# Loading all token tiles at once and reordering the opening of a fused recurrent, attention and expert block

## The chip, the cores and the metric

The kernel runs on one core of a Trainium2 chip. A core has five instruction queues: TensorE (PE in the profile, with its weight loads as PEld), VectorE (DVE), ScalarE (ACT), GpSimd (POOL) and SyncE (SP, which here only issues DMAs). The metric is the device time of one execution in microseconds, the median of three runs.

## The reference, cut to what matters

One layer over 1024 tokens of width 1024, in float32:

```python
u = rms_norm(h, norm_mix_g)
proj = u @ w_in                 # 1024 x 5152
x_rnn, g_rnn, q_c, kv_c, k_pe, gate_logits = split(proj)
A = rg_lru(causal_conv(x_rnn)) * gelu(g_rnn)
B = mla(q_c, kv_c, k_pe, positions)      # rope on a part of q and k
h = h + (sigmoid(gA) * A + sigmoid(gB) * B) @ w_out
h = h + hier_moe(rms_norm(h))            # top-2 of 8 experts in the best of 4 groups
```

The change touches only the opening: reading h, normalizing it, the first columns of `u @ w_in`, and the cosine and sine tables that rope uses later.

## The kernel before

Every float32 operand of a matmul is held as a high and a low part: `split` casts the value to the short form on ScalarE and subtracts the cast from the value on VectorE. A product is three matmuls (high by high, low by high, high by low). The instructions are put in order per engine by a list scheduler: program order is the priority among those that are ready, and each engine then runs its list strictly in that order. `tc.issue_after(i)` adds one constraint to that: what the block traces on the engine of `i` stands behind `i` in that engine's list.

**The opening (L332 to L396).** The tokens come in eight tiles of 128 rows. `load_x` fetches one tile (SP queue) into one of four buffers `xt`, so tile 4 waits until tile 0 has been scaled. `prepare` squares and sums it on ScalarE (L343) and takes the reciprocal root with a dozen tiny VectorE instructions (`rsqrt`, L80 to L87). `turn_tile` scales the tile by root and gain (L353 on VectorE; for tiles 5 and 7 L350 on ScalarE and L351 on GpSimd), transposes it on TensorE in eight blocks (L358), and splits it into `uh` and `ul` (both at L96). From tile 2 on the transposes share one PSUM buffer, tag `po`.

**The three begun projections.** `begin` loads 128 columns of `w_in` and splits them; for the first two the subtraction runs on GpSimd (`by=G`). `start_part(c0, q)` runs the 24 matmuls of 128x256 (L164) of one projection over the tokens of tiles 2q and 2q+1. The order is: for each q, projection 0, a tile, projection 1, a tile, projection 2. So quarter q of all three waits for tiles 2q and 2q+1. The last quarter runs in `proj_ft`.

**The rope tables (`rope_tables`, L284 to L330).** They are 27 VectorE instructions, nearly all in one chain, on 128x128 numbers or fewer, one transpose on TensorE and two sines on ScalarE. They stand in program order behind the first two `prepare` calls. Their scratch pool `wR` is released after the opening.

**What follows.** Scratch pool `wS` takes the place of `wR` and of the opening's pool; its last buffer, `tz`, covers nearly all of what `wR` held. The rest of the latent projections run (L169 to L171, then k_pe at L505, small sums at L476 and L512), while VectorE builds the Strassen sums of `u` (`u_sums`, L207 to L215 and L96), 28 instructions of 128x1024 that begin when tile 7 is split. Their results `t1` to `t4` are the operands of the products in `pair` (L245), which begin behind L512. `t1h`, `t1l`, `t2h`, `t2l` have 8 KB per partition each and are unused before that.

Of the kernel before, what the change touches and what calls it, by code (L numbers as in the profile page):

```python
# [10 lines left out]
F32 = mybir.dt.float32  # L11
F32R = mybir.dt.float32r
BF16 = mybir.dt.bfloat16
I32 = mybir.dt.int32
AF = mybir.ActivationFunctionType
OP = mybir.AluOpType
# [3 lines left out]
P = 128  # L20
T = 1024
D = 1024
NT = T // P
# [15 lines left out]
def block_kernel(ctx: ExitStack, tc, a, out):  # L39
    nc = tc.nc  # L40
    V, S, G, TE = nc.vector, nc.scalar, nc.gpsimd, nc.tensor
# [4 lines left out]
    def bcast_row(ap1, n):  # L46
        return bass.AP(tensor=ap1.tensor, offset=ap1.offset, ap=[[0, P], [1, n]])
# [25 lines left out]
    def rsqrt(dst, src, shape, pool):  # L73

        n = int(np.prod(shape))
        view = lambda t: t if len(shape) == 1 else t.rearrange("p (a b) -> p a b", a=shape[0])
        gi = pool.tile([P, n], I32, tag=f"rsi{n}", name="rs_i")
        tt = pool.tile([P, n], F32, tag=f"rst{n}", name="rs_t")
        g3, t, y = view(gi), view(tt), view(gi.bitcast(F32))
        V.tensor_scalar(g3, src.bitcast(I32), 1, -1, op0=OP.arith_shift_right, op1=OP.bitwise_xor)  # L80
        V.tensor_tensor(gi, gi, magic[:, :n], op=OP.add)
        if n == 1:
            hs = pool.tile([P, 1], F32, tag="rsh", name="rs_h")
            V.tensor_scalar(hs, src, -0.5, None, op0=OP.mult)
            for it in range(3):
                V.scalar_tensor_tensor(t, y, y, hs, op0=OP.mult, op1=OP.mult)
                V.scalar_tensor_tensor(dst if it == 2 else y, t, 1.5, y, op0=OP.add, op1=OP.mult)  # L87
            return
        for it in range(3):
            V.tensor_tensor(t, y, y, op=OP.mult)  # L90
            V.scalar_tensor_tensor(t, t, -0.5, src, op0=OP.mult, op1=OP.mult)
            V.scalar_tensor_tensor(dst if it == 2 else y, t, 1.5, y, op0=OP.add, op1=OP.mult)

    def split(hi, lo, src, by=V):

        return S.copy(hi, src), by.tensor_tensor(lo, src, hi.bitcast(F32), op=OP.subtract)  # L96
# [13 lines left out]
    up = tc.alloc_tile_pool(name="up", bufs=1, reuse_waits="tile")  # L110
    uh = [up.tile([P, KD, 512], F32R, name=f"uh{i}") for i in range(2)]
    ul = [up.tile([P, KD, 512], F32R, name=f"ul{i}") for i in range(2)]
    K4 = KD // 2
    psW = tc.alloc_tile_pool(name="psW", bufs=3, space=PSUM, reuse_waits="tile")
# [10 lines left out]
    def bank(nm="ps"):  # L125
        return bank2(nm)[:, 0] if psA is None else psA.tile([P, 512], F32, tag="ps", name=nm)
# [20 lines left out]

    begun = {}

    def proj_weights(c0, by=V):  # L150
        st = raw_tile().rearrange("p (k f) -> p k f", k=KD)
        nc.sync.dma_start(st, w_in_v[:, :, c0:c0 + P])
        b0 = 3 + 2 * (turn[2] % 3)
        turn[2] += 1
        wh, wl = (new(b0 + n, F32R).rearrange("p (k f) -> p k f", k=KD) for n in range(2))
        split(wh, wl, st, by)
        return wh, wl

    def proj_part(ps, w, hf, sl):
# [13 lines left out]
    def proj_ft(c0, done):  # L173
        if c0 in begun:
            ps, w = begun.pop(c0)
            proj_part(ps, w, 1, slice(256, 512))
        else:
            w = proj_weights(c0)
            ps = bank2()
            proj_half(ps, w, 0)  # L180
            proj_half(ps, w, 1)
        done(ps.rearrange("p h t -> p (h t)"))
# [8 lines left out]
    ub = {}  # L191

    def u_sums(pool):

        for nm in ("t1", "t2", "t3"):
            ub[nm] = tuple(up.tile([P, K4, 512], F32R, name=f"{nm}{q}") for q in "hl")
        for nm, h, k in (("b11", 0, 0), ("b21", 0, K4), ("b22", 1, K4), ("t4", 1, 0)):
            ub[nm] = tuple([t[h][:, k:k + K4] for t in (uh, ul)])
        b12 = ub["t4"]
        f = lambda t, s: t[:, s].bitcast(F32)  # L200
        for k in range(0, K4, 2):
            s = slice(k, k + 2)
            tmp = lambda nm: pool.tile([P, 2, 512], F32, tag=nm, name=nm, bufs=1)

            def minus(nm, a, b):
                x, y = tmp(nm), tmp("ty")
                V.tensor_tensor(x, f(a[0], s), f(b[0], s), op=OP.subtract)  # L207
                V.tensor_tensor(y, f(a[1], s), f(b[1], s), op=OP.subtract)
                V.tensor_tensor(x, x, y, op=OP.add)
                return x  # L210

            def less(nm, a, x):
                y = tmp(nm)
                V.tensor_tensor(y, f(a[0], s), x, op=OP.subtract)
                V.tensor_tensor(y, y, f(a[1], s), op=OP.add)  # L215
                return y

            x3 = minus("tx", ub["b22"], b12)
            split(*(t[:, s] for t in ub["t3"]), x3)
            x1 = minus("tz", b12, ub["b11"])  # L220
            split(*(t[:, s] for t in ub["t1"]), x1)
            x2 = less("tx", ub["b22"], x1)
            split(*(t[:, s] for t in ub["t2"]), x2)
            x4 = less("tz", ub["b21"], x2)
            split(*(t[:, s] for t in ub["t4"]), x4)
# [56 lines left out]
    wR = tc.alloc_tile_pool(name="wR", bufs=1, side="right", reuse_waits="tile")  # L282

    def rope_tables(w0):  # L284
# [5 lines left out]
        gqk = w0.tile([P, 2, DQ], F32, name="gqk")  # L290
        for i, nm in enumerate(("q_norm_g", "k_norm_g")):
            nc.scalar.dma_start(gqk[:, i, :], bcast_row(a[nm], DQ))
        pp2 = bank("pp2")[:, :NT]
        TE.transpose(pp2, posf, ident[:NT, :NT])
        pos = w0.tile([P, NT], F32, name="pos")
        V.tensor_copy(pos, pp2)
# [35 lines left out]
    with tc.tile_pool(name="wA", bufs=4, side="right", reuse_waits="tile") as wA:  # L332
        gmix = wA.tile([P, D], F32, name="gmix", bufs=1)
        xts, rs = {}, {}

        def load_x(i):
            xts[i] = wA.tile([P, D], F32, tag="xt", name="xt")
            nc.sync.dma_start(xts[i], x[i * P:(i + 1) * P, :])

        def prepare(i):  # L340
            ss, rs[i] = (wA.tile([P, 1], F32, tag=nm, name=nm) for nm in ("ss", "rs"))
            xns[i] = wA.tile([P, D], F32, tag="xn", name="xn")
            S.activation(xns[i], xts[i], AF.Square, scale=D ** -0.5, accum_out=ss)  # L343
            V.tensor_scalar(ss, ss, EPS, None, op0=OP.add)
            rsqrt(rs[i], ss, [1], wA)

        def turn_tile(i, tag):
            xn, r = xns[i], rs[i]
            if i % 2 and i > 3:
                S.activation(xn, xts[i], AF.Copy, scale=r)  # L350
                G.tensor_tensor(xn, xn, gmix, op=OP.mult)  # L351
            else:
                V.scalar_tensor_tensor(xn, xts[i], r, gmix, op0=OP.mult, op1=OP.mult)  # L353
            hh, ii = divmod(i, 4)
            pt = psW.tile([P, 2, 512], F32, tag=tag, name="pt", bufs=1 if tag == "po" else 3)
            pt = pt.rearrange("p h (c t) -> p (h c) t", c=4)
            for k in range(KD):
                TE.transpose(pt[:, k], xn[:, k * P:(k + 1) * P], ident)  # L358
            split(uh[hh][:, :, ii * P:(ii + 1) * P], ul[hh][:, :, ii * P:(ii + 1) * P], pt)

        def begin(c0, by):
            begun[c0] = [None, proj_weights(c0, by=by)]

        def start_part(c0, q):
            if begun[c0][0] is None:
                begun[c0][0] = psW.tile([P, 2, 512], F32, tag="ps", name="pp")
            proj_part(*begun[c0], q // 2, slice(256 * (q % 2), 256 * (q % 2) + 256))

        xns = {}
        first = (C_Q, C_Q + P, C_Q + 2 * P)  # L370
        load_x(0)
        load_x(1)
        nc.sync.dma_start(gmix, bcast_row(a["norm_mix_g"], D))
        for i in range(2):
            prepare(i)
        begin(first[0], G)
        rope_tables(wR)
        for i in range(2):
            turn_tile(i, "ps")
            load_x(2 + i)  # L380
        for i in range(2, 4):
            prepare(i)
        begin(first[1], G)
        begin(first[2], V)
        for i in range(4, NT):
            load_x(i)
        for q in range(3):
            for n, c0 in enumerate(first):
                start_part(c0, q)
                if n < 2:  # L390
                    turn_tile(2 * q + 2 + n, "po")
            if q < 2:
                for i in range(2):
                    prepare(2 * q + 4 + i)

    wR.release()  # L396

# [81 lines left out]
    with tc.tile_pool(name="wS", bufs=2, side="right", reuse_waits="tile") as wS:  # L479
# [20 lines left out]
        ps = bank2()  # L500
# [17 lines left out]
    with tc.tile_pool(name="wD", bufs=1, side="right", reuse_waits="tile") as wD:  # L518
# [7 lines left out]
        for fp in range(4):  # L526
            fs = [2 * fp, 2 * fp + 1]
            c0 = 2 * P * fp
# [4 lines left out]
            for j, ft in enumerate(fs):  # L533
                y = wD.tile([P, T], F32, tag="y", name="y", bufs=2)
# [19 lines left out]
            for j, ft in enumerate(fs):  # L554
                for w in range(2):
                    ps = [bank("psl") for _ in range(2)]
# [1037 lines left out]
```

## Time and profile before

| | |
|---|---|
| time, three runs | 1417.18, 1420.1, 1422.19 us (median 1420.1) |
| the profiled execution | 1418.82 us, its span 1417.1 us |
| busy in the span | PE 95%, PEld 77%, DVE 77%, ACT 55%, POOL 27% |
| mean granted TensorE clock | 0.979 |

The span is what the engines recorded; 1.7 us lie around it. A group of rows below is one view of that one execution, with times in microseconds from the start of the span. Instructions on one engine overlap a little: a 128x1024 VectorE instruction that lasts 1.22 is followed by the next 1.13 later.

### The profile page before, as it was taken

To read this page: it belongs to the slowest core of one execution; us is meant where nothing else is said; L and a number is where in the kernel's file an instruction comes from. 1 tells how busy PE (TensorE), PEld (TensorE's weight loads), DVE (VectorE), ACT (ScalarE), POOL (GpSimd) and SP (SyncE) were. 2 spreads that over 40 slices of the span, in tenths; PEclk is the share of its full clock that TensorE was granted. 3 is DMA by queue.
4 is the path that set the end of the run, shared out by engine and by line. 5 is a ranking of instruction groups with operands and counts; after the bars stand their busy time and mean duration, and the time that the engine had idled before them with its cause. 6 is when DMAs were issued, how large, how long until landed. Compare 5 with 4: busy or idle time off the path is not lost.

```text
span 1417.1 us, 20382 instructions
## 1 busy us (share of the span) xinstructions
PE 1344.1 (95%) x7371; PEld 1094.3 (77%) x7372; DVE 1090.0 (77%) x1894; ACT 783.0 (55%) x1138; POOL 382.0 (27%) x313
## 2 busy tenths in 40 slices
PE   5999999999999899998999999998995999999995
PEld 4967888888888788987655555557874999999995
DVE  7698878787966655678577777785496899999894
ACT  5444747565734353423444444444532888888884
POOL 2100000000000211221777777550422222222222
PEclk9999999999999899999999999999997999999998
DMA  6112222222353545643434444363567899999962
GB/s 216 49 59 87 89 75 89 75 90 89 134 178 120 178 173 172 174 148 99 116 100 117 107 120 132 107 220 134 198 233 250 289 379 381 380 380 379 368 175 36
DMA packets 119945, 244.32 MB, mean 172 GB/s; under 512 B 32636, under 2 KB 68564, under 8 KB 119840
## 3 DMA queue, kind: packets, MB, share of 16 engines
q1 hardware_dynamic: 101768, 194.37, 40.9%
q0 software_dynamic: 17616, 48.46, 11.1%
q8 instruction: 59, 0.97, 0.3%
q14 instruction: 46, 0.38, 0.1%
q10 hardware_dynamic: 456, 0.14, 0.0%
HBM read 203.87 MB, written 55.83 MB: 183 GB/s over the span
## 4 chain that ended last, share of the span: by engine, by line
PE 83%; DVE 11%; DMA 2%; ACT 2%; issue 1%; POOL 0%; SPq 0%; POOLq 0%; DVEq 0%; ACTq 0%
PE pw L245 22%; PE pg L1442 13%; PE po L971 6%; PE py L1479 6%; PE pq L787 6%; PE ph L1172 4%; PE psm L923 3%; PE psl L560 3%; PE pss L953 3%; PE pss L955 2%; PE pss L954 2%; PE pt L1424 2%; PE pp L164 2%; PE pk L705 2%; PE pv L764 1%; DVE s L96 1%
## 5 line engine op out<-in xcount | busy, mean ns | idle before, releaser
L96 ACT CAST s<-s 128x1024 fp32r<-128x1024 f32 (+4 forms) x392 | 337.9, 882 | 179.8 <-PE pw L245 39.7
L96 DVE TENSOR_TENSOR s<-s,s 128x1024 fp32r<-128x1024 f32 (+3 forms) x384 | 382.5, 1023 | 52.8 <-ACT s L96 47.4
L1442 PE MATMUL pg<-s,s 128*128 128x256 f32 x1536 | 196.3, 284 | 0.7 <-DVE s L96 0.7
L1442 PEld LDWEIGHTS pg<-s,s 128*128 128x128 f32 x1536 | 189.8, 191 | 3.5 <-DVE s L96 0.9
L245 PE MATMUL pw<-uh,s 128*128 128x512 f32 x576 | 183.0, 392 | 0.0
L956 ACT ACTIVATE s<-pss 128x512 f32<-128x512 f32 (+4 forms) x192 | 90.1, 493 | 148.6 <-PE pss L955 144.9
L976 POOL TENSOR_TENSOR s<-s,s 128x896 f32<-128x896 f32 (+6 forms) x108 | 149.8, 1406 | 58.3 <-ACT s L956 40.8
L245 PEld LDWEIGHTS pw<-uh,s 128*128 128x128 f32 x576 | 108.8, 189 | 23.9 <-ACT s L96 0.9
L924 DVE TENSOR_REDUCE mx<-psm 128x1 f32<-128x320 f32 (+4 forms) x192 | 94.5, 547 | 41.1 <-PE psm L923 40.7
L245 PE MATMUL pw<-ul,s 128*128 128x512 f32 x288 | 112.7, 391 | 0.0
L971 PE MATMUL po<-s,s 128*64 128x512 f32 (+3 forms) x384 | 106.8, 507 | 0.3 <-ACT s L956 0.3
L1172 PE MATMUL ph<-s,s 128*128 128x512 f32 x384 | 98.3, 404 | 3.5 <-ACT s L96 2.9
L787 PE MATMUL pq<-s,cqh 128*128 128x384 f32 x384 | 99.2, 337 | 0.0
L1479 PE MATMUL py<-s,hT 128*128 128x512 f32 x384 | 96.2, 399 | 1.2 <-ACT hT L96 1.2
L1485 POOL DMA_INDIRECT out_dram<-s,idx x32 | 54.7, 1709 | 121.6 <-ACT s L1484 107.4
L1172 PEld LDWEIGHTS ph<-s,s 128*128 128x128 f32 x384 | 70.6, 191 | 19.5 <-ACT s L96 4.1
L1479 PEld LDWEIGHTS py<-s,hT 128*128 128x128 f32 x384 | 69.8, 188 | 15.1 <-ACT hT L96 1.4
L953 PE MATMUL pss<-s,s 128*128 128x512 f32 (+4 forms) x192 | 72.9, 380 | 3.0 <-ACT s L956 3.0
L1416 POOL DMA_INDIRECT s<-xs,idx x32 | 35.7, 1117 | 131.2 <-PE pt L1424 107.1
L953 PEld LDWEIGHTS pss<-s,s 128*128 128x128 f32 x192 | 36.4, 189 | 44.0 <-DVE mx L924 17.0
L787 PEld LDWEIGHTS pq<-s,cqh 128*128 128x128 f32 x384 | 69.2, 188 | 1.1 <-DVE vt L768 0.8
L955 PE MATMUL pss<-s,s 128*128 128x512 f32 (+4 forms) x192 | 65.8, 343 | 0.0
(389 smaller groups left out, 2603.8 us busy)
## 6 DMA issues: line engine op xcount, KB each, us to landing
s<-in_w_gate_dram SPq DMA_DIRECT2D x64, 512.0 KB
s<-in_w_up_dram SPq DMA_DIRECT2D x63, 512.0 KB
s<-in_w_down_dram SPq DMA_DIRECT2D x63, 512.0 KB
s<-in_w_in_dram SPq DMA_DIRECT2D x40, 512.0 KB
s<-rk_d SPq DMA_DIRECT2D x16, 384.0 KB
q_d<-qt POOLq DMA_DIRECT2D x8, 768.0 KB, 4.7
s<-q_d SPq DMA_DIRECT2D x16, 384.0 KB
s<-in_w_uq_dram SPq DMA_DIRECT2D x12, 384.0 KB
```

The source lines that it names most:

```text
L96: return S.copy(hi, src), by.tensor_tensor(lo, src, hi.bitcast(F32), op=OP.subtract)
L245: TE.matmul(ps[at], w[:, l, k], ub[b][m][:, k], start=(go and k == 0 and n == 0), stop=(k == K4 - 1 and n == 2), skip_group_check=True)
L787: TE.matmul(p2[:, t % 2, :384], l[:, k, i * P:(i + 1) * P], wq[k // 2][r][:, k % 2], start=(k == 0 and n == 0), stop=(k == 5 and n == 2))
L924: V.tensor_reduce((mx[:, j, R1 + i:R1 + i + 1], mx2[:, j, i:i + 1])[b], ps[:, :cn], axis=AX.X, op=OP.max, negate=True)
L953: TE.matmul(o[:, :cn], kh[:, ks], qh[:, q], start=True, stop=False)
L955: TE.matmul(o[:, :cn], kh[:, ks], ql[:, q], start=False, stop=True)
L956: S.activation(pT[:, b * cn:(b + 1) * cn], o[:, :cn], AF.Exp)
L971: TE.matmul(po[pp][s][j * DV:(j + 1) * DV, lo - s * 512:], va[:, c, j, :], pTs[j][:, lo - c * P:hi - c * P], start=(c == 0), stop=(c == 4 ...
L976: (V if pp == NP - 1 and j == 0 and c < 5 else G).tensor_tensor(ac, ac, pTs[j][:, :T - c * P], op=OP.add)
L1172: TE.matmul(o, m2[l][:, k], wo[c][k // 2][r][:, k % 2], start=(k == 0 and m == 0), stop=(k == KD - 1 and m == 2))
L1442: TE.matmul(pg[:, u], l[:, k], r, start=(k == 0 and m == 0), stop=(k == KD - 1 and m == 2))
L1479: TE.matmul(py[hf], l[:, k, :], wd[k][w][:, hf * 512:(hf + 1) * 512], start=(k == 0 and m == 0), stop=(k == 1 and m == 2))
```

## The change

- The eight token tiles are loaded in pairs into the four Strassen buffers `t1h` to `t2l`, without a wait for a buffer. The four buffers `xt` are gone.
- No arithmetic on GpSimd: the subtractions of the first two weight tiles, and the gain of tiles 5 and 7, run on VectorE. For tiles 5 and 7 the separate scaling on ScalarE is gone.
- `begin` only loads; the splitting is in `begin_split`. Loads are issued early, and the splits are placed behind given instructions.
- Both first reciprocal roots stand ahead of the first scaling; the squares of tiles 2 and 3 stand behind the cast of tile 0; the splits of the second and third weight tile stand behind those of tile 1.
- The VectorE part of the rope tables stands behind the last tile's subtraction. Their transpose uses PSUM tag `po`.

```diff
--- before.py
+++ after.py
@@ -84,8 +84,8 @@
             V.tensor_scalar(hs, src, -0.5, None, op0=OP.mult)
             for it in range(3):
                 V.scalar_tensor_tensor(t, y, y, hs, op0=OP.mult, op1=OP.mult)
-                V.scalar_tensor_tensor(dst if it == 2 else y, t, 1.5, y, op0=OP.add, op1=OP.mult)
-            return
+                r = V.scalar_tensor_tensor(dst if it == 2 else y, t, 1.5, y, op0=OP.add, op1=OP.mult)
+            return r
         for it in range(3):
             V.tensor_tensor(t, y, y, op=OP.mult)
             V.scalar_tensor_tensor(t, t, -0.5, src, op0=OP.mult, op1=OP.mult)
@@ -147,13 +147,16 @@
 
     begun = {}
 
-    def proj_weights(c0, by=V):
+    def proj_raw(c0):
         st = raw_tile().rearrange("p (k f) -> p k f", k=KD)
         nc.sync.dma_start(st, w_in_v[:, :, c0:c0 + P])
+        return st
+
+    def proj_weights(st):
         b0 = 3 + 2 * (turn[2] % 3)
         turn[2] += 1
         wh, wl = (new(b0 + n, F32R).rearrange("p (k f) -> p k f", k=KD) for n in range(2))
-        split(wh, wl, st, by)
+        split(wh, wl, st)
         return wh, wl
 
     def proj_part(ps, w, hf, sl):
@@ -175,7 +178,7 @@
             ps, w = begun.pop(c0)
             proj_part(ps, w, 1, slice(256, 512))
         else:
-            w = proj_weights(c0)
+            w = proj_weights(proj_raw(c0))
             ps = bank2()
             proj_half(ps, w, 0)
             proj_half(ps, w, 1)
@@ -193,7 +196,7 @@
     def u_sums(pool):
 
         for nm in ("t1", "t2", "t3"):
-            ub[nm] = tuple(up.tile([P, K4, 512], F32R, name=f"{nm}{q}") for q in "hl")
+            ub[nm] = tuple(up.tile([P, K4, 512], F32R, tag=f"{nm}{q}", name=f"{nm}{q}") for q in "hl")
         for nm, h, k in (("b11", 0, 0), ("b21", 0, K4), ("b22", 1, K4), ("t4", 1, 0)):
             ub[nm] = tuple([t[h][:, k:k + K4] for t in (uh, ul)])
         b12 = ub["t4"]
@@ -290,7 +293,7 @@
         gqk = w0.tile([P, 2, DQ], F32, name="gqk")
         for i, nm in enumerate(("q_norm_g", "k_norm_g")):
             nc.scalar.dma_start(gqk[:, i, :], bcast_row(a[nm], DQ))
-        pp2 = bank("pp2")[:, :NT]
+        pp2 = psW.tile([P, 2, 512], F32, tag="po", name="pp2", bufs=1)[:, 0, :NT]
         TE.transpose(pp2, posf, ident[:NT, :NT])
         pos = w0.tile([P, NT], F32, name="pos")
         V.tensor_copy(pos, pp2)
@@ -334,7 +337,9 @@
         xts, rs = {}, {}
 
         def load_x(i):
-            xts[i] = wA.tile([P, D], F32, tag="xt", name="xt")
+            if i % 2 == 0:
+                t = up.tile([P, 2, D], F32, tag=("t1h", "t1l", "t2h", "t2l")[i // 2], name="xt")
+                xts[i], xts[i + 1] = t[:, 0], t[:, 1]
             nc.sync.dma_start(xts[i], x[i * P:(i + 1) * P, :])
 
         def prepare(i):
@@ -342,46 +347,52 @@
             xns[i] = wA.tile([P, D], F32, tag="xn", name="xn")
             S.activation(xns[i], xts[i], AF.Square, scale=D ** -0.5, accum_out=ss)
             V.tensor_scalar(ss, ss, EPS, None, op0=OP.add)
-            rsqrt(rs[i], ss, [1], wA)
+            return rsqrt(rs[i], ss, [1], wA)
 
         def turn_tile(i, tag):
             xn, r = xns[i], rs[i]
-            if i % 2 and i > 3:
-                S.activation(xn, xts[i], AF.Copy, scale=r)
-                G.tensor_tensor(xn, xn, gmix, op=OP.mult)
-            else:
-                V.scalar_tensor_tensor(xn, xts[i], r, gmix, op0=OP.mult, op1=OP.mult)
+            scaled.append(V.scalar_tensor_tensor(xn, xts[i], r, gmix, op0=OP.mult, op1=OP.mult))
             hh, ii = divmod(i, 4)
             pt = psW.tile([P, 2, 512], F32, tag=tag, name="pt", bufs=1 if tag == "po" else 3)
             pt = pt.rearrange("p h (c t) -> p (h c) t", c=4)
             for k in range(KD):
                 TE.transpose(pt[:, k], xn[:, k * P:(k + 1) * P], ident)
-            split(uh[hh][:, :, ii * P:(ii + 1) * P], ul[hh][:, :, ii * P:(ii + 1) * P], pt)
-
-        def begin(c0, by):
-            begun[c0] = [None, proj_weights(c0, by=by)]
+            turned[:] = split(uh[hh][:, :, ii * P:(ii + 1) * P], ul[hh][:, :, ii * P:(ii + 1) * P], pt)
+
+        def begin(c0):
+            begun[c0] = [None, proj_raw(c0)]
+
+        def begin_split(c0):
+            begun[c0][1] = proj_weights(begun[c0][1])
 
         def start_part(c0, q):
             if begun[c0][0] is None:
                 begun[c0][0] = psW.tile([P, 2, 512], F32, tag="ps", name="pp")
             proj_part(*begun[c0], q // 2, slice(256 * (q % 2), 256 * (q % 2) + 256))
 
-        xns = {}
+        xns, turned, scaled = {}, [], []
         first = (C_Q, C_Q + P, C_Q + 2 * P)
         load_x(0)
         load_x(1)
         nc.sync.dma_start(gmix, bcast_row(a["norm_mix_g"], D))
+        begin(first[0])
+        r1 = [prepare(i) for i in range(2)][1]
         for i in range(2):
-            prepare(i)
-        begin(first[0], G)
-        rope_tables(wR)
-        for i in range(2):
-            turn_tile(i, "ps")
+            with tc.issue_after(r1.ins):
+                turn_tile(i, "ps")
             load_x(2 + i)
-        for i in range(2, 4):
-            prepare(i)
-        begin(first[1], G)
-        begin(first[2], V)
+            if i == 0:
+                cast0 = turned[0]
+        begin(first[1])
+        begin(first[2])
+        with tc.issue_after(scaled[1].ins):
+            begin_split(first[0])
+        with tc.issue_after(cast0.ins):
+            for i in range(2, 4):
+                prepare(i)
+        with tc.issue_after(turned[0].ins), tc.issue_after(turned[1].ins):
+            begin_split(first[1])
+            begin_split(first[2])
         for i in range(4, NT):
             load_x(i)
         for q in range(3):
@@ -392,6 +403,8 @@
             if q < 2:
                 for i in range(2):
                     prepare(2 * q + 4 + i)
+        with tc.issue_after(turned[1].ins):
+            rope_tables(wR)
 
     wR.release()
 
```

## Rows read from the trace of the kernel before

**Rows 1.** The page: busy share in 40 slices, and the chain by engine

```profile
...
PE   5999999999999899998999999998995999999995
...
PE 83%; DVE 11%; DMA 2%; ACT 2%; issue 1%; POOL 0%; SPq 0%; POOLq 0%; DVEq 0%; ACTq 0%
...
```

**Rows 2.** PE's waits, 0 to 120 us: total us, times, longest

```profile
...
PE pt L358 <- DVE xn L353: 7.6, 3, 6.8
PE pp L164 <- ACT uh L96: 3.7, 2, 2.4
...
```

**Rows 3.** Windows: busy us of each engine (xcount), granted clock, DMA share, GB/s

```profile
...
20.00:25.00 5.00, 4.28 (x35) 4.28 (x36) 5.00 (x26) 2.71 (x6) 0.00 (x0) 1.00 0.53 120
...
30.00:35.00 5.00, 2.63 (x16) 2.39 (x15) 3.24 (x13) 3.10 (x5) 0.00 (x0) 0.75 0.23 84
35.00:40.00 5.00, 5.00 (x28) 5.00 (x28) 5.00 (x22) 1.17 (x2) 2.36 (x1) 0.57 0.00 0
...
45.00:50.00 5.00, 5.00 (x44) 5.00 (x44) 0.99 (x1) 0.00 (x0) 0.00 (x0) 1.00 0.01 3
...
```

**Rows 4.** Chain of waits, 20 to 66 us: start, us, what

```profile
...
25.96 5.10 DMA xt<-in_x_dram
...
31.15 1.15 ACT xn L343 x2
...
33.24 5.49 PE pp L164 x24
38.74 1.21 PE pt L358 x8
39.94 2.87 PE pp L164 x24
42.81 0.87 PE pt L358 x8
...
57.04 8.63 PE pp L164 x72
...
```

**Rows 5.** Timeline, all engines, 0 to 45 us: start, us, engine, line

```profile
...
13.36 1.86 DVE L312 SCALAR_TENSOR_TENSOR ang<-kf,ang 128x128 f32<-128x128 f32 x1
...
15.96 3.42 PE L164 MATMUL pp<-uh,s 128*128 128x256 f32 x16 [1.30 <-ACT uh L96]
...
16.93 2.38 POOL L96 TENSOR_TENSOR s<-s,s 128x1024 fp32r<-128x1024 f32 x1 [1.87 <-ACT s L96]
16.99 2.33 DVE L86 SCALAR_TENSOR_TENSOR rs_t<-rs_i,rs_h 128x1 f32<-128x1 f32 x1
...
20.72 1.22 PE L164 MATMUL pp<-ul,s 128*128 128x256 f32 x8 [1.33 <-DVE ul L96]
...
27.32 1.27 DVE L353 SCALAR_TENSOR_TENSOR xn<-xt,rs,gmix 128x1024 f32<-128x1024 f32 x1
...
```

**Rows 6.** Timeline, all engines, 35 to 75 us

```profile
...
36.81 3.47 DVE L353 SCALAR_TENSOR_TENSOR xn<-xt,rs,gmix 128x1024 f32<-128x1024 f32 x1
...
55.14 1.23 DVE L96 TENSOR_TENSOR ul<-pt,uh 128x1024 fp32r<-128x1024 f32 x1 [2.52 <-ACT uh L96]
...
```

**Rows 7.** Timeline, DVE, inside the rope tables

```profile
...
23.12 0.28 DVE L329 TENSOR_TENSOR tS<-cs,gqk 128x128 f32<-128x128 f32 x1
23.32 0.21 DVE L320 TENSOR_SCALAR fl<-ang 128x128 f32<-128x128 f32 x1
...
```

**Rows 8.** Timeline, DVE, the end of the Strassen sums

```profile
...
98.06 1.22 DVE L96 TENSOR_TENSOR ul<-tz,uh 128x1024 fp32r<-128x1024 f32 x1
...
```

**Rows 9.** Timeline, PE, in the first pairs

```profile
...
98.58 0.50 PE L245 MATMUL pw<-t2h,s 128*128 128x512 f32 x1 [1.43 <-ACT s L96]
...
124.48 0.50 PE L560 MATMUL psl<-yh,s 128*128 128x512 f32 x1 [0.67 <-DVE o L264]
...
```

**Rows 10.** DVE's waits, 56 to 125 us, all of them

```profile
...
DVE ul L96 <- ACT uh L96: 2.5, 1, 2.5
DVE kp L513 <- PE kp L512: 0.6, 1, 0.6
...
```

## The prediction

> **What bounds the kernel now.** I read the page first. TensorE is busy nearly everywhere, and the chain that ended last runs through it for 83% of the span and through VectorE for 11% [rows 1]. The first of the 40 slices is the exception: there PE is half idle. What is saved there counts in full only if PE never has to wait again for something that did not move with it. So there are two questions: how much earlier can PE run in the opening, and which engine sets the pace behind it?
>
> *The opening.* PE's waits over the first 120 us name the scaled token tile (7.6 us in three waits) and the cast of a tile (3.7 us in two) [rows 2]. The windows show why: from 20 to 25 us VectorE is full, 5.00 of 5.00, while PE is not. From 30 to 35 us PE has work for 2.63 of 5 us, and from there to 40 us its granted clock is 0.75 and then 0.57, that is, it runs much of the time at the lower of its two levels, 1.2 of 2.4 GHz, although it is busy [rows 3]. The chain of waits gives the piece in between. Tiles 6 and 7 are loaded only at 25.96, when buffers come free; ScalarE squares them at 31.15, ahead of the cast of tile 3, which stands behind them in its list; PE starts the second quarter of the projections at 33.24. The first 24 matmuls then take 5.49 and the eight transposes 1.21, against 2.87 and 0.87 for the same work right afterwards [rows 4]. From there to the end of the begun projections at 65.67 PE has no gap.
>
> VectorE is also held up while GpSimd computes: a reciprocal-root step of 0.21 lasts 2.33, ending with the GpSimd subtraction beside it, and a rope step of 0.28 lasts 1.86 [rows 5]. A scaling of 1.27 lasts 3.47 in the time of a later GpSimd product [rows 5, 6].
>
> *Behind the opening.* Tile 7 is split from 55.14 on [rows 6], and right behind it VectorE begins the Strassen sums. The last of them starts at 98.06 [rows 8]. PE has meanwhile come to the products that need them: it waits 1.43 at 98.58, and again 0.67 at 124.48 for VectorE [rows 9]. Between tile 7 and 125 us VectorE itself waits 0.6 in all, apart from the wait for tile 7's own cast [rows 10]. So from 56 to 125 us VectorE sets the pace, with PE close behind: PE's whole reserve in these 60 us is about the 2.1 it waits.
>
> **The change part by part.**
>
> *No GpSimd arithmetic.* Four GpSimd instructions become VectorE ones: two subtractions (1.22 each, as the one in [rows 8]) and two scalings (1.27 each), 5.0 in all. What goes are the hold-ups: 2.33 - 0.21, 1.86 - 0.28 and 3.47 - 1.27, together 5.9 [rows 5, 6]. So this nearly cancels on VectorE, 0.9 to the good; the bounds are all of 5.0 lost, if those instructions fall where VectorE is full, and all of 5.9 gained.
>
> The Trainium skill speaks against this edit: Perfetto Trace Analysis, Optimizing Scalar/DVE Operations, says that with a saturated DVE moving work to ScalarE or even GpSimd may make sense, and adds that the two share a port, so that moving between them might not help. By its first half the sum would be worse by 5.0; by its second half it would be about nothing, which is what the three stretched instructions here bear out.
>
> *Tables moved out, roots first, loads at once.* The first part of projection 0 starts at 15.96, behind tile 1's transposes and cast. These are not faster, since PE's first sixteen transposes take what they take, so I leave 15.96. Its second half then no longer waits until 20.72 for a subtraction that a GpSimd hold-up delayed [rows 5]: 24 matmuls take 3.42 + 1.22 = 4.6 and end at 20.6 instead of 21.9. With the tables gone from VectorE and tiles 2 and 3 squared early, two tiles at 0.87 and two parts at 2.87 follow without a gap: 20.6 + 7.5 = 28.1, and 0.2 for the single transpose buffer, 28.3. Tile 3's cast no longer stands behind a late load. So the second quarter starts 33.24 - 28.3 = 4.9 earlier. PE has no pause ahead of it, so its first part and transposes run at the higher level: (5.49 - 2.87) + (1.21 - 0.87) = 3.0 [rows 4]. Together **7.9** at the split of tile 7, and at the end of the begun projections. Bounds: 7.9 - 5.0 = 2.9, if the new VectorE work delays tiles 2 and 3 in full, and 8.8 with the 0.9. The loads cost nothing: the new buffers are unused until the sums, and the DMA engines are idle from 35 us on [rows 3]; without that cover the last tile's 5.10 would show [rows 4].
>
> *The tables behind tile 7.* Before, they lay in the opening. Now their 27 VectorE instructions stand at the head of the stretch where VectorE sets the pace, while the idle VectorE time ahead of tile 7 (from 45 to 50 us it works 0.99 of 5) stays unused [rows 3]. By the code 16 of them are of the 0.28 kind, 10 of the 0.21 kind and one is 0.16: 6.7 laid end to end. Packed between other work the next one starts 0.20 after one of 0.28 [rows 7], an overlap of 0.08, so 6.7 - 27 x 0.08 = 4.6. That is the lower bound. The chain also leaves VectorE for one transpose and two sines, and the sums cannot fill all the gaps: their buffer `tz` lies where the tables' scratch lay, so from the fourth sum on they wait until the tables are done. Each trip to another engine may cost up to the 2.5 that VectorE waited for ScalarE just before [rows 10]; with both sines exposed that is 6.7 + 5.0 = 11.7, the upper bound. I take **5.6**, one above the packed figure, because four sums and a weight split are there to fill the gaps. Behind the waiting tables stand the sums, and for them wait the products on PE.
>
> *Behind that.* PE arrives at the small sums 7.9 earlier, so VectorE's wait of 0.6 for them goes [rows 10]: **0.6** gained. PE now reaches the products some 5 us before their sums and waits there. After such a pause its matmuls may run at the lower level again: up to 2.6, as in 24 matmuls at 5.49 [rows 4], but mostly inside a stretch in which it waits for VectorE anyway. I take **0.4** lost. Behind 125 us the order is the old one and everything shifts.
>
> **The sum.** 7.9 - 5.6 + 0.6 - 0.4 = 2.5 us gained. The profiled execution took 1418.8 (span 1417.1 and 1.7 around it), so 1416.3; it lies 1.3 below the median of the runs, 1420.1. Against the median: **1417.6**. The runs before spread over 5 us, so a difference under 0.3%, 4.3 us, can hardly be told from none.
>
> **The rivals.**
>
> *The opening's gain survives.* If the tables hide in VectorE's gaps, or PE finds other products to do while it waits, the 7.9 reaches the end: 1412.2. For it: VectorE is nearly idle just ahead of tile 7 [rows 3], and the scheduler may reorder products. Against it: VectorE's 0.6 of waits in 70 us [rows 10], and each product needs its weights split on the same VectorE.
>
> *The tables' chain becomes the new wait.* If the sines are exposed in full (11.7), the sums start 11.7 - 7.9 = 3.8 later than before, less 0.6; PE waits for them, and falls to the lower clock at 2.6: 5.8 slower, 1425.9. It decides from the point at which the tables end more than 8.5 after tile 7's split. For it: `tz` keeps the sums from covering the chain, and ScalarE has the latent projections' squares and copies in its list at just that time. Against it: the chain needs only 6.7 of VectorE.
>
> *The opening is not as fast as planned.* With 5.0 more on VectorE in its full stretch, 20 to 25 us [rows 3], only 2.9 is gained and 5.6 - 0.6 + 0.4 lost: 2.5 slower, 1422.6. Against it: the 5.9 of hold-ups go with the same edit. This is what the first half of the rule above would make of it (the Trainium skill, Perfetto Trace Analysis, Optimizing Scalar/DVE Operations).
>
> **Chances.** The forecast 0.45, the surviving gain 0.27, the exposed chain 0.18, the slow opening 0.10. Of the first, about a seventh falls below 1415.8; of the second nearly all; of the exposed chain about three quarters lies above 1424.4, and some of the slow opening. That makes faster 0.30, same 0.52, slower 0.18. The range reaches from 1411.0, just beyond the surviving gain, to 1425.5, which leaves the worst of the exposed chain out; the forecast's own range is 1415 to 1420.
>
> **What would show it.** Right: the second quarter of the projections starts near 28 instead of 33.24, with no slow matmuls behind it; tile 7's subtraction at about 47; the tables' instructions right behind it, ending near 55; the last sum near 95.5; a PE wait of some 5 us or more on the sums between 80 and 97; then PE's order as before. Wrong: tiles 2 and 3 still scaled after 24; sums that end 6 or more earlier than 98, which is the first rival; tables that end 9 or more after tile 7, which is the second; or a difference that arises behind 125 us, where I expect none.

## The result, and the profile after

The changed kernel takes 1429.81 us (median of 6 runs, 1427.87 to 1433.15) against 1420.28 for the kernel before (median of 6 as well): the ratio is 1.0071, with a 95% interval from 1.0054 to 1.0087. It is about 10 us slower. Forecast was 1417.6, 2.5 faster than the median before, and the range ended at 1425.5. The profiled execution has a span of 1426.1, 9.0 more than that of before. In the new code the projections, the rope tables, the sums and the pairs stand 3 lines further down than in the old one (L245 is now L248), the squares 5 (L348), the scaling and the transposes 1 (L354, L359), and all behind the opening 13.

The page of the changed kernel, busy share and granted clock in 40 slices, and the chain by engine:

```profile
...
PE   5969999999999899998999999998985999999995
...
PEclk9979999999999989999999999999997999999998
...
PE 83%; DVE 10%; DMA 2%; ACT 2%; issue 1%; POOL 0%; SPq 0%; POOLq 0%; ACTq 0%; DVEq 0%
...
```

One digit tells where to look: the third slice, 71 to 107 us, has PE at 6 and its clock at 7, where the row of before shows 9 [rows 1]. The waits of PE from 0 to 120 us name the cause:

```profile
...
PE pw L248 <- DVE s L96: 13.0, 1, 13.0
PE pt L359 <- DVE xn L354: 11.1, 1, 11.1
PE pp L167 <- ACT uh L96: 4.8, 2, 3.9
PE ps L172 <- ACT cq L504: 1.3, 1, 1.3
```

The first row is new, a single wait of 13.0. It doesn't name one of the Strassen sums. It names `s L96`, the low part of a weight. (The second row is the wait for the very first tile. In [rows 2] its longest, 6.8, is the same wait, shorter there because the transpose of the rope tables stood ahead of it.) The windows that answer to [rows 3], and one over the new wait:

```profile
...
20.00:25.00 5.00, 5.00 (x38) 5.00 (x37) 5.00 (x23) 3.60 (x6) 0.00 (x0) 0.84 1.09 326
30.00:35.00 5.00, 4.02 (x34) 3.82 (x33) 5.00 (x20) 2.06 (x3) 0.00 (x0) 1.00 0.00 0
35.00:40.00 5.00, 5.00 (x45) 5.00 (x44) 4.34 (x8) 1.70 (x2) 0.00 (x0) 1.00 0.00 0
45.00:50.00 5.00, 5.00 (x46) 5.00 (x45) 1.23 (x1) 1.32 (x2) 0.00 (x0) 1.00 0.00 0
80.00:97.00 17.00, 5.38 (x46) 4.01 (x38) 17.00 (x17) 5.09 (x5) 0.00 (x0) 0.69 0.12 31
...
```

The opening did get better: PE works 4.02 of 5 us from 30 to 35 instead of 2.63, and at clock 1.00 from 30 on instead of 0.75 and 0.57. From 80 to 97, however, it works 5.38 of 17 while VectorE is full. The chain of waits, in order of time (start, us, what), shows where the opening and the pairs wait:

```profile
...
11.75 3.89 DMA prow<-in_lru_bx_dram
...
31.53 3.13 PE pp L167 x24
34.66 0.87 PE pt L359 x8
...
57.00 1.28 ACT L326
58.30 0.32 ACT cs L326
...
97.12 0.60 DVE s L256
97.72 0.61 DVE s L96
98.38 35.31 PE pw L248 x144
...
```

And the timeline, with the instructions that these steps consist of:

```profile
...
12.44 0.31 ACTq L426 DMA_DIRECT2D prow<-in_q_a_g_dram  x1
13.71 0.24 ACTq L426 DMA_DIRECT2D prow<-in_kv_a_g_dram  x1
15.30 0.28 ACTq L426 DMA_DIRECT2D prow<-in_norm_ffn_g_dram  x1
...
15.62 1.01 ACT L96 CAST uh<-pt 128x1024 fp32r<-128x1024 f32 x1 [3.51 <-DMA prow<-in_lru_bx_dram]
...
18.64 1.65 PE L167 MATMUL pp<-uh,s 128*128 128x256 f32 x6 [3.86 <-ACT uh L96]
...
50.73 1.22 DVE L96 TENSOR_TENSOR ul<-pt,uh 128x1024 fp32r<-128x1024 f32 x1 [2.52 <-ACT uh L96]
51.88 0.20 DVE L292 CAST posf<-posi 8x128 f32<-8x128 int32 x1
...
57.02 1.23 DVE L96 TENSOR_TENSOR s<-s,s 128x1024 fp32r<-128x1024 f32 x1 [0.52 <-ACT s L96]
...
61.60 0.28 DVE L331 TENSOR_TENSOR tC<-cs,gqk 128x128 f32<-128x128 f32 x1
61.80 1.22 DVE L210 TENSOR_TENSOR tx<-uh 128x1024 f32<-128x1024 f32 x1
...
64.66 0.64 ACT L96 CAST s<-s 128x512 fp32r<-128x512 f32 x1
...
97.63 0.69 DVE L96 TENSOR_TENSOR s<-s,s 128x512 fp32r<-128x512 f32 x1
98.24 1.22 DVE L96 TENSOR_TENSOR ul<-tz,uh 128x1024 fp32r<-128x1024 f32 x1
...
98.38 1.22 PE L248 MATMUL pw<-uh,s 128*128 128x512 f32 x2 [12.99 <-DVE s L96]
...
```

For comparison, three lines from the trace of the kernel before: the first pair's difference `a21` and its first two low halves on VectorE, and the third matmul of that pair on PE.

```profile
...
80.17 0.68 DVE L253 TENSOR_TENSOR s<-s 128x512 f32<-128x512 f32 x1
...
83.04 1.28 DVE L96 TENSOR_TENSOR s<-s,s 128x512 fp32r<-128x512 f32 x2
...
88.13 1.05 PE L245 MATMUL pw<-uh,s 128*128 128x512 f32 x2
...
```

Read the changed kernel's lines from the top. Tile 0's cast starts at 15.62 because it stands in ScalarE's list behind eight issues of small loads (`prow`, the rows of constants), the last two of which come late; PE's first part starts at 18.64 instead of 15.96 [rows 5]. Tile 7 is split at 50.73 instead of 55.14 [rows 6], 4.4 earlier. The tables then take VectorE from 51.88 to 61.88, 10.0 us, with one weight split (57.02) and four small copies but no sum among them, so the first sum starts at 61.80. Yet the last instruction of the sums starts at 98.24, and in the kernel before it started at 98.06 [rows 8]. The sums are hardly later at their end, because the work on the first pair's weights, which stood among them before, now comes behind their last addition. The subtraction at 97.63 is part of it: the first pair's first product needs this low half, PE takes its products in the order of its list, and so one subtraction of 0.69 holds PE for 13.0. Its input was not late: the first cast of a weight of this size ran on ScalarE at 64.66.

In the kernel before PE began the first pair's products at 87.1. Now it begins at 84.7, does the two matmuls that need only the weight's high half, to 85.39, and goes on with the third at 98.38. That is 98.38 - 88.13 = 10.3 later at the same place. The waits of 1.43 and 0.67 [rows 9] are gone in return, which leaves 8.2. The last matmul of all the pairs starts at 488.5 instead of 480.0, 8.5 later; the 0.3 between is not traced. Behind it nothing is won or lost beyond half a microsecond.

### The profile page after: what moved, and what is told of

The parts are those of the page before. It is cut to its first block, busy times and chain, and to the rows that moved or that the text cites. A ratio compares the mean times of both kernels' runs of the same rounds, so it can differ in the third digit from the quotient of the medians.

```text
span 1426.1 us, 20370 instructions
## 1 busy us (share of the span) xinstructions
PE 1342.9 (94%) x7371; PEld 1094.0 (77%) x7372; DVE 1092.5 (77%) x1898; ACT 780.5 (55%) x1136; POOL 371.2 (26%) x309
## 4 chain that ended last, share of the span: by engine, by line
PE 83%; DVE 10%; DMA 2%; ACT 2%; issue 1%; POOL 0%; SPq 0%; POOLq 0%; ACTq 0%; DVEq 0%
PE pw L248 24%; PE pg L1455 13%; PE po L984 6%; PE py L1492 6%; PE pq L800 6%; PE ph L1185 3%; PE psm L936 3%; PE psl L573 3%; PE pss L966 3%; PE pss L968 2%; PE pss L967 2%; PE pp L167 2%; PE pt L1437 2%; PE pk L718 2%; PE pv L777 1%; DVE s L96 1%
## 5 line engine op out<-in xcount | busy, mean ns | idle before, releaser
L96 ACT CAST s<-s 128x1024 fp32r<-128x1024 f32 (+4 forms) x392 | 337.9, 882 | 184.9 <-PE pw L248 43.4
L96 DVE TENSOR_TENSOR s<-s,s 128x1024 fp32r<-128x1024 f32 (+3 forms) x386 | 385.5, 1026 | 55.0 <-ACT s L96 49.6
L248 PE MATMUL pw<-uh,s 128*128 128x512 f32 x576 | 183.6, 393 | 13.0 <-DVE s L96 13.0
L248 PEld LDWEIGHTS pw<-uh,s 128*128 128x128 f32 x576 | 109.0, 189 | 37.3 <-DVE s L96 13.4
L248 PE MATMUL pw<-ul,s 128*128 128x512 f32 x288 | 112.8, 392 | 0.0
```

The lines of the kernel that those rows point to most:

```text
L248: TE.matmul(ps[at], w[:, l, k], ub[b][m][:, k], start=(go and k == 0 and n == 0), stop=(k == K4 - 1 and n == 2), skip_group_check=True)
```

## The experiments

All ran five rounds against the kernel before. "Ratio" is to that kernel, with its 95% interval; where a difference is given in us, it is worked out from the ratio times 1420, and is uncertain by 1 to 2.5 us; a difference between two changed versions is uncertain by 2 to 3 us. The theory (A in most of the expectations): the tables behind tile 7 make the whole loss, by delaying the sums and by a changed order of VectorE's list. The rival: the loss comes from the other parts, the opening's DMAs and the work taken from GpSimd.

**Only the tables put back.** The changed kernel with the tables where they were, behind the first two roots:

```
+        rope_tables(wR)
...
-        with tc.issue_after(turned[1].ins):
-            rope_tables(wR)
```

> The changed kernel with only the rope tables back where they stood, behind the first two reciprocal roots and without a pin; all else of the change stays. Theory A (the tables behind tile 7 are the cause: VectorE begins the Strassen sums at 61.8 instead of 56.3, and the weights of the first products are split only behind all sums): the sums begin at 56 or before, PE's wait of 13.0 at 98 us goes, and the time falls from 1429.8 to 1420 or below, down to about 1417. Theory B (the opening itself is the loss: four more VectorE instructions, ScalarE's list held by small DMAs): at least half of the 9.5 stays, 1425 or more.

Measured: 1419.19, ratio 0.9991 (0.9983 to 1.0). With the tables back nothing of the loss is left, so the remaining edits together are worth about 1 us. PE's waits from 60 to 140 us in this run:

```profile
...
PE psl L572 <- DVE o L267: 0.7, 1, 0.7
PE pw L248 <- DVE kp L525: 0.5, 1, 0.5
PE pw L248 <- ACT s L96: 0.4, 1, 0.4
```

**Only the tables moved.** The kernel before, with the tables alone behind tile 7's split:

```
-        rope_tables(wR)
...
+        with tc.issue_after(turned[1].ins):
+            rope_tables(wR)
```

> The kernel before with one part of the change alone: the rope tables' VectorE part behind tile 7's subtraction, their transpose on the other PSUM tag. Loads, GpSimd arithmetic and order are those of before. Theory A: slower than before by about as much as the whole change or more, 1428 to 1434, with the first products' weight splits behind all sums as in the changed kernel. Theory B: within 3 us of before, 1417 to 1423.

Measured: 1429.3, ratio 1.0061 (1.0048 to 1.0074), and the same wait in PE's list from 60 to 140 us:

```profile
...
PE pw L245 <- DVE s L96: 12.7, 1, 12.7
...
```

One move alone (the tables, and with them the PSUM tag of their transpose) reproduces the loss, with the GpSimd work and the four buffers in place. Tile 7 is split at 50.76 here, within 0.1 of the full change: moving the tables out is enough for the faster opening too.

**The tables in the idle stretch.** The changed kernel with the tables pinned behind tile 5's subtraction instead of tile 7's, where VectorE has little to do:

```
+            if q == 1:
+                with tc.issue_after(turned[1].ins):
+                    rope_tables(wR)
```

> The changed kernel with the rope tables pinned behind tile 5's subtraction instead of tile 7's, so that they run in VectorE's nearly idle time ahead of tiles 6 and 7. Theory A: the sums begin right behind tile 7, near 51 to 52, the first products' weights are split in time, and the 4.4 that the opening gained reaches the products: 1414 to 1418, faster than both kernels. Theory B: no better than the tables in the old place. A third theory (the sums are not what PE waits for): unchanged, 1429.

Measured: 1417.64, ratio 0.9982 (0.9973 to 0.9991), 2.6 faster than before and 12.6 faster than the change: theory A, at the slow end of its range. Tile 7's split comes at 52.04, 1.3 later than in the change, since tile 6's subtraction stands behind a piece of the chain (48.59 instead of 46.99) and holds the one transpose buffer; the first sum starts at 53.18 instead of 61.80.

**The weights first, tables still late.** The changed kernel, with the first pair's loads, differences and first three weight splits written ahead of the sums, so that they have priority over them:

```
+        pair_open(C_X)
         u_sums(wS)
```

> The changed kernel with the tables where it has them (behind tile 7), but with the weight splits of the first pair's first three products (a11, a12, a21) ahead of the Strassen sums in program order, and so in priority. Theory A1 (the late tables cost about 5.5 by themselves and the rest of the 9 comes from the order that the list scheduler then chose for the splits): PE's single wait of 13.0 breaks up, its three products (8 us of PE work) run during it, and 3 to 4 us come back: 1425 to 1427. Theory A2 (the tables alone account for all of it, since the sums' end sets the pace): within 1 us of 1429.8.

Measured: 1422.44, ratio 1.0011 (1.0002 to 1.0019): 8.5 of the 10 come back with the tables where the change put them. This is outside both ranges, far more than I expected, and it showed that the order is the larger part of the loss. The wait of 13.0 is replaced by small ones, although the last instruction of the sums starts only at 103.10. That is where they end when the weights keep their place among them, 5.0 later than before:

```profile
...
PE pw L273 <- DVE s L96: 1.4, 3, 0.9
PE ps L172 <- ACT cq L527: 1.3, 1, 1.3
PE pw L273 <- ACT o L281: 1.3, 1, 1.3
PE pw L273 <- DVE t2l L96: 0.8, 1, 0.8
```

**The order alone, tables early.** The opposite corner: tables at their old place, but the first pair's difference `a21` and the subtractions of its weight splits pinned behind the last addition of the sums:

```
+        late = lambda: tc.issue_after(summed.ins) if early else nullcontext()
...
+            with late():
                 V.tensor_tensor(w[:, 1], a, w[:, 0].bitcast(F32), op=OP.subtract)
...
+        with late():
             V.tensor_tensor(a21, a11, a21, op=OP.subtract)
```

> The changed kernel with the tables back at their old place behind the first two roots (1419.2 so), and the first pair's a21 difference and its weight splits on VectorE pinned behind the last addition of the sums: the order that the changed kernel got by itself, without late tables. Theory A (that order alone makes the long wait): the last addition ends near 94, the splits follow, TensorE waits once for about 8 instead of in three waits of 0.5 to 0.7, at a lower granted clock behind it, time 1425 to 1428. Rival B (the order costs little as the sums end 3 earlier without the splits among them and the products then run through without a wait): 1419 to 1421, and the whole loss of the change is in the tables' chain.

Measured: 1427.7, ratio 1.0047 (1.0033 to 1.0061). PE waits once, as foretold, and the timeline of VectorE shows the last addition at 92.63, `a21`, the split, and only then the last sum's subtraction. The wait is shorter than the change's 13.0, as the last addition starts 3.3 earlier than there (92.63 against 95.90):

```profile
...
PE pw L254 <- DVE s L249: 8.9, 1, 8.9
...
```

```profile
...
92.63 1.22 DVE L219 TENSOR_TENSOR tz<-tz,ul 128x1024 f32<-128x1024 f32 x1
93.77 0.68 DVE L263 TENSOR_TENSOR s<-s 128x512 f32<-128x512 f32 x1
94.37 0.68 DVE L249 TENSOR_TENSOR s<-s,s 128x512 fp32r<-128x512 f32 x1
94.97 1.22 DVE L97 TENSOR_TENSOR ul<-tz,uh 128x1024 fp32r<-128x1024 f32 x1
...
```

So a square of four can be filled, in us against the kernel before:

| | weights among or ahead of the sums | weights behind the sums |
|---|---|---|
| tables early, at the old place | -1.3 | +6.7 |
| tables behind tile 7 | +1.6 | +10.1 (the change) |

The order costs 8.0 in one row and 8.5 in the other; the tables' place itself 2.9 and 3.4. Within their uncertainty the two add up.

**Both repairs.** Tables in the idle stretch and weights first:

> The changed kernel with the tables pinned behind tile 5's subtraction and the first pair's first weight splits written ahead of the sums. Beside the run with the weights first and the tables late (1422.4) only the tables' place differs, and beside the run with the tables in the gap (1417.6) only the weights' order. Theory A (two separate costs: late tables some 5, weights behind the sums some 7.4, and the second only where the tables are late, since with early tables the list has the splits among the sums anyway): 1416.5 to 1419, so the tables' place alone is worth 3.5 to 6. Rival B (the order is nearly all of it and the tables' place worth 2 or less): 1420.5 to 1422.

Measured: 1415.98, ratio 0.9965 (0.9952 to 0.9979), 5.0 faster than before. Against the run with the weights first and the tables late the tables' place alone is now worth 6.6, a little over theory A's 3.5 to 6; rival B is out. The timeline of VectorE shows the tables from 42.63 on, mostly in idle time, and the first sum at 53.50:

```profile
...
42.63 0.20 DVE L315 CAST posf<-posi 8x128 f32<-8x128 int32 x1
...
51.24 0.28 DVE L354 TENSOR_TENSOR tC<-cs,gqk 128x128 f32<-128x128 f32 x1
52.35 1.23 DVE L96 TENSOR_TENSOR ul<-pt,uh 128x1024 fp32r<-128x1024 f32 x1 [0.83 <-ACT uh L96]
53.50 1.22 DVE L210 TENSOR_TENSOR tx<-uh 128x1024 f32<-128x1024 f32 x1
...
```

**The small loads.** The changed kernel, tables late, with the loads of the constants pinned behind tile 1's cast on ScalarE:

```
+        with tc.issue_after(cast1.ins):
             nc.scalar.dma_start(prow[r0:r0 + n, :], src)
```

> The changed kernel, tables still behind tile 7, with one thing more: the twelve small loads of the row constants on ScalarE's list (prow) are pinned behind tile 1's cast, so that tile 0's cast no longer stands behind them. Theory A (those loads hold the whole opening back by 2.6, since TensorE is the bound from tile 2 on): tile 0's cast at 13.0 instead of 15.62, the second quarter of the projections at 28.9 instead of 31.53, tile 7's subtraction at 48.1 instead of 50.73, and as VectorE is the bound from there to the first pair's weights, the time falls by 2.6 to 1427.2. Rival B (something else stands next in the opening, the token loads or VectorE's normalizations, as the kernel before with only its tables late also reached tile 7 at 50.76 with its first cast at 13.04): the cast comes early, tile 7's subtraction stays at 50 to 51, and the time at 1429 to 1430.

Measured: 1426.55, ratio 1.004 (1.0026 to 1.0053), 4.4 below the change by the ratios and 3.3 by the medians: theory A. Its 2.6 lies within the uncertainty of that difference. Tile 0's cast now starts at 12.99 and tile 7's split at 47.52, 3.2 earlier than in the change. The wait in the pairs is the same 13.0; all of it has only moved forward.

```profile
...
12.99 1.01 ACT L96 CAST uh<-pt 128x1024 fp32r<-128x1024 f32 x1 [1.15 <-PE pt L359]
...
```

**The small loads with the tables in the idle stretch:**

> The changed kernel with the tables pinned behind tile 5's subtraction (as in the run with the tables in the idle gap, 1417.6) and the small loads of the row constants pinned behind tile 1's cast. Theory A: the 2.6 of the opening comes on top, tile 7's subtraction at 49.4 instead of 52.04, last sum some 2.5 earlier at 92.4, TensorE's waits before the first pair's products shrink, time 1415.0. Rival B: the opening stays bound by something else, time 1417 to 1418. Rival C: VectorE's sums come earlier but TensorE is busy with the second half of the projections and the latents up to 84 anyway, so that a third to a half of it is kept: 1416 to 1417.

Measured: 1415.1, ratio 0.9961 (0.9947 to 0.9974), 5.5 faster than before and 2.9 by the ratios below the run without the pinned loads: theory A, though its interval touches rival C. This is the fastest version by the ratio, with no clear distance to the others around it.

**All three repairs:**

> The changed kernel with all three repairs: the tables pinned behind tile 5's subtraction, the first pair's first weight splits written ahead of the sums, the small loads of the row constants pinned behind tile 1's cast. Theory A (the opening's 2.6 is passed on in full where TensorE waits no more than 0.9 before 120): 2 to 3 below the run with the gap and the weights first, 1413 to 1414.5. Rival B (VectorE's sums are the limit of either): the same as the two runs with two of the three, 1415 to 1416.

Measured: 1415.55, ratio 0.9974 (0.9963 to 0.9986): no gain over two of the three, rival B. Beside the run with the gap and the weights first, PE begins the pairs at 81.4 instead of 84.7, but its last pair matmul starts at 474.6 against 475.5, so 3.3 shrink to 0.9 on the way, in part by waits for weights (1.6 against 0.7). Behind the pairs this execution loses more: its span is 1414.7 against 1412.1. That is no more than executions of one kernel differ by here. What takes the rest I have not traced.

**One part alone each.** The kernel before with only the loads at once, and with only GpSimd's arithmetic moved to VectorE:

```
+            if i % 2 == 0:
+                t = up.tile([P, 2, D], F32, tag=("t1h", "t1l", "t2h", "t2l")[i // 2], name="xt")
+                xts[i], xts[i + 1] = t[:, 0], t[:, 1]
```

> The kernel before with one part of the change alone: the eight token tiles are loaded at once into the space of the sums instead of through four buffers; tables, GpSimd's part and the order stay as they were. Theory A (no tile was late in the kernel before but for its computation, as the kernel before with only its tables late reached tile 7's subtraction at 50.76, within 0.1 of the changed kernel, with its four buffers): tile 7's subtraction stays near 55, time 1419.5 to 1421.5. Rival B (the loads of tiles 4 to 7 move earlier and take DMA time from the first projections' weights): tile 7's subtraction 1 to 3 later, 1421.5 to 1424. Rival C: a gain of 1 to 3, 1417 to 1419.

Measured: 1418.27, ratio 0.9992 (0.998 to 1.0003): no difference that can be told, with a visible one in the opening. Tile 7's split comes at 52.54 instead of 55.14, 2.6 earlier, against theory A; the time lies in rival C's range, but its interval holds no gain as well. No load stands in the chain from 20 to 66 us any more; a small step of VectorE that takes 2.29 of it, as those in [rows 5], stands there:

```profile
...
36.01 2.29 DVE rs_i L87
...
```

```
-            if i % 2 and i > 3:
-                S.activation(xn, xts[i], AF.Copy, scale=r)
-                G.tensor_tensor(xn, xn, gmix, op=OP.mult)
...
-        begin(first[0], G)
+        begin(first[0], V)
...
-        begin(first[1], G)
+        begin(first[1], V)
```

> The kernel before with one part of the change alone: the weight splits of the first two projections' columns and the normalization of tiles 5 and 7 on VectorE instead of GpSimd (and ScalarE); loads, tables and order stay as they were. Theory A (the prediction's: 5.0 of VectorE's work added, 5.9 of its hold-ups beside GpSimd removed): 1418.5 to 1421.5. Rival B (the longer VectorE list delays the tables' chain and the normalizations behind it): second quarter of the projections after 34, time 1422 to 1425. Rival C: the hold-ups were in the chain and the added work is not: second quarter before 31, time 1415 to 1418.

Measured: 1421.4, ratio 1.0012 (1.0001 to 1.0023), 1.7 slower, with 0.1 to 3.3 in the interval. The time lies in theory A's range, the opening is rival B's: the second quarter starts at 34.23, 1.0 later than before [rows 4], and its first 24 matmuls still take 5.49. The hold-ups did go: no VectorE instruction ahead of 56 us lasts longer than 1.3. But a weight's subtraction (11.84) now stands ahead of tile 1's scaling (13.56), and PE's first part starts at 17.96 instead of 15.96. So with 5.0 added and 5.9 of hold-ups gone the kernel is not 0.9 faster, as the prediction reckoned for VectorE, but 1.7 slower. The Trainium skill (Perfetto Trace Analysis, Optimizing Scalar/DVE Operations) leaves open whether moving work between VectorE and GpSimd helps, as they share a port. By this run undoing such a move costs 1.7 of 5.0, nearer to its second half than to its first, though the interval reaches past the middle.

## Why the prediction was wrong

*The step that failed* is the one behind the tables: "PE now reaches the products some 5 us before their sums and waits there", priced at 0.4, with "PE's order as before". It took VectorE's list behind tile 7 as given and moved it as a block. The list is written by the scheduler from what is ready when. In the kernel before, the first pair's `a21` difference and its first two low halves stood among the sums (0.68 at 80.17 and 1.28 at 83.04 us). In all three kernels that have the tables late and the sums first in program order (the change, the tables moved alone, the small loads pinned), these stand behind the last addition. PE's long wait is not for a sum, but for a weight that in the kernel before was made 15 us earlier. This is 8.0 to 8.5 of the miss, shown by both rows of the square. The whole miss is 12.6, from 2.5 faster to 10.1 slower; the other 4 lie in the next two terms, since with the order mended and the tables late the kernel is still 1.6 slower and not 2.5 faster. Why the scheduler put the weights last stays open; the runs show that it did, and what that cost.

*The tables* were mis-sized: 5.6 forecast, 10.0 measured on VectorE from tile 7's split to the first sum, or some 8.8 without the weight split of 1.2 among them, which had to be done in any case. I assumed that four sums and a weight split would fill the chain's gaps. One weight split did; no sum stood among the tables in the list. The gaps are the transpose (0.63), the load of the sine's table on ScalarE (1.28) ahead of the first sine, and the chain's own steps, each some 0.3 apart instead of the packed 0.20. The upper bound, 11.7, was nearer. Yet where the order was good the late tables cost only 2.9 at the end, though the first sum started 7.1 later (62.43 with the weights first, 55.32 with the tables put back): the delay of VectorE behind tile 7 is not passed on in full.

*The opening* was over-sized: 7.9 forecast, 4.4 measured. The slow matmuls did go (24 in 3.13, transposes in 0.87: 2.7 of the 3.0). The second quarter, however, starts at 31.53 and not 28.3, because the first part did not stay at 15.96. I counted the instructions that leave and not those that move up: on ScalarE the small loads of the constants came ahead of tile 0's cast, which starts at 15.62. The tables' move alone doesn't do that: with only the tables moved the cast starts at 13.04, and with all of the change but the tables' move it starts at 13.02. It takes both. Pinning the loads gave 4.4 and 2.9 us in two runs, each uncertain by 2 to 3, and nothing in the run with all three repairs.

*GpSimd's part* was put at about nothing: 1.7 slower alone, inside the bounds, with the added work ahead of tile 1's scaling. *Loads that cost nothing*: right, with a small gain in the opening that the tables' move gives as well.

*The rival that came nearest* is "the tables' chain becomes the new wait", 1425.9. Its sign and its clue were right (the tables end at 61.88, 9.9 after the end of tile 7's split, beyond the 8.5 from which it decides; PE waits and its granted clock falls to 0.69), its mechanism was not: the sums' last instruction starts 0.2 later than before, and PE waits for a weight.

## What to carry over

Where an engine's list is written by a scheduler, a moved block changes the order of everything that it competed with. Before pricing the move, ask which small instruction the next engine needs first, and whether anything holds it ahead of the long block; here 0.69 of VectorE's work held PE for 13.0, and naming it ahead of the sums won 8.5. Work that only needs to be done by some time belongs into the stretch where its engine is idle: ahead of tile 7 the tables cost little, behind it they held the sums up by 10.0. And compare the end of a delayed stretch as well as its start: the sums began 5.5 later and ended 0.2 later, so something else had left their stretch, and that gives the changed order away.

## What the runs showed of the hardware

An issue of a load on ScalarE's list can hold that engine up: five issues stand 0.3 apart from 11.08 to 12.44, the next two follow only at 13.71 and 15.30, and the cast behind them starts 3.51 after ScalarE's last work. With these loads out of the way it starts at 12.99. Five of them ahead of the cast did no harm in the run with the tables put back, where it starts at 13.02; why the last two come late, no run shows.

Behind its wait of 13.0 PE ran at the lower of its two clock levels (1.2 of 2.4 GHz): the granted clock was 0.51 from 98.4 to 103.6 us and 1.00 from 104 to 110. Two matmuls took 1.22 at 98.38, and 0.62 at 104.28. The wait is not the only thing that leads there. In the kernel before, the first products behind the small sums ran at 0.52 from 88.1 to 90.6 too, with no wait ahead of them.
